# Six raw-weight buffers and three split pairs in place of four and four, in a one-core decoder layer kernel

## The chip, the cores and the metric

The kernel runs on one core of one Trainium2 chip. A time is the device time of one execution in microseconds (us). The core has a matrix engine (PE, with its weight loads listed apart as PEld), a vector engine (DVE), a scalar engine (ACT), a general engine (POOL), and a sync engine (SP) that does little but issue DMA transfers. ACT issues some transfers too.

## What is computed

One layer of a hybrid decoder, 1024 new tokens and 8 sample tokens of width 2048, in float32:

```python
mod = jax.nn.silu(c) @ w_ada + b_ada
shift, scale, gate = jnp.split(mod[:, None, :], 3, axis=-1)
h = rmsnorm(x, norm_g) * (1.0 + scale) + shift
z = h @ w_in                                   # 2048 x 8208
b_a, c_a, h_a, g_a, qkv, g_b, beta_logit, alpha_logit = jnp.split(z, SPLIT_POINTS, axis=-1)
conv_out, new_a_buf = causal_depthwise_conv(c_a * h_a, conv_a_buf, conv_a_w)
y_a = b_a * conv_out * jax.nn.silu(g_a)
...
o, s = gated_delta_rule(q, k, v, g, beta, s0)  # chunks of 64, a triangular solve in each
o = rmsnorm(o, o_norm_g).reshape(bsz, t, D_GDN).astype(x.dtype) * jax.nn.silu(g_b)
y = jnp.concatenate([y_a, o], axis=-1) @ w_out
return x + gate * y, ...                       # then a final rmsnorm
```

## The kernel before, in words

**Tiles and halves.** The tokens are taken in two halves: half 0 has 512 tokens, half 1 has 512 and the 8 samples, worked as blocks of 264 and 256 columns. In each half `h @ w_in` is made first, together with the convolution groups and the DeltaNet heads, then `@ w_out`, the residual (`res`) and the norm.

**The weight stream.** The weights come as 672 pieces of 512 rows by 128 columns (256 KB): 0 to 255 are `w_in` in half 0, 256 to 319 `w_out` in half 0, 320 to 575 `w_in` in half 1, 576 to 671 `w_out` in half 1. Class `Stream` (object `ws`, line 565 on) takes each through three steps. SP loads it into a `raw` buffer. ACT copies it to `whi` in the reduced format fp32r, and POOL or DVE (function `split_w`, which takes POOL if the planner has it free) subtracts that from `raw` into `wlo`. PE then multiplies the piece in three passes, `hh`·`whi`, `hl`·`whi` and `hh`·`wlo`, where `hh` and `hl` are the two parts of the activations (`yhi`, `ylo` in the out-projection); a piece is 12 matmuls of 512 columns, or 24 of 264 and 256; 64 pieces of the last out-projection (576 to 607 and 640 to 671) have 12 of 264 or 256 alone. `RAW` (line 391) says how many `raw` buffers there are, `SPL` how many pairs of `whi` and `wlo`. A load may be issued when it is fewer than `RAW` pieces ahead of the last split, a split when it is fewer than `SPL` ahead of the pieces that PE has finished with (method `ahead`, line 603).

**The ramp.** At the start the first two thirds of `w_ada` (shift and scale) are needed. They are 64 tiles `wat` of 512 KB, with `ADA` = 9 buffers. SP's queue issues nine of them, then `ws.ahead(0)` issues the first four raw pieces, and from then on the two kinds alternate as buffers come free. PE makes the matrix-vector products of each tile (`matvec`, tiles `tpt<-wat,sc`), `spread` transposes their result (`tpt<-cs,ev`), ACT and DVE make `hh` and `hl` of the rows that it opens, and in the waits for tiles PE does matmuls of the first 28 pieces (`first_products`, into seven PSUM tiles `mm`, `tpt`, `cht`, `ot`; `fill` takes as many as fit). While `ws.eager` is true (the ramp) the stream keeps this order; `od.spawn(ws.run())` ends it.

**The order of the work.** All instructions go through `_Order` (object `od`), a planner with a cost of each instruction and transfer; generators run beside the products (the DeltaNet `chain`, the samples, the norms) and each is continued when the planner's clock for PE reaches its due time. This runs when the kernel is built. It settles the order of the instructions on every engine, and on the chip each engine works its list in that order. So a change of the buffers also moves DVE, ACT and POOL work of other parts.

**The solve and the PSUM.** Each DeltaNet head has a triangular solve: a matrix goes to DRAM (`ub`), comes back as `tb` by a transfer that ACT issues (512 KB), and DVE does 31 steps of `ob` and `xb` with it. DVE also empties the PSUM tiles `mm` of the products (`y<-y,mm`, `ua<-c_,mm`, `res<-mm`), of which there are three; PE can't begin a product until a tile is empty.

All operations are recorded in two helpers, so every DVE, ACT, POOL and DMA row has line 321 and every matmul line 370; rows are told apart by their tiles.

Of the kernel before, what the change touches and what calls it, by code (L numbers as in the profile page):

```python
# [77 lines left out]
def trunk_kernel(tc, xT, w_in, w_ada, w_out, pack, consts, vecs, csq, ssm,  # L78
                 yT, cap, cqp, ssp, cas, cqs, sss):
    nc = tc.nc  # L80
    ctx = ExitStack()
    with ctx:
        _trunk(ctx, tc, nc, xT, w_in, w_ada, w_out, pack, consts, vecs, csq, ssm, yT, cap, cqp, ssp, cas, cqs, sss)
# [6 lines left out]
class _Order:  # L90
# [156 lines left out]
    def pump(self):  # L247
        for s in list(self.side):
            if s[0] <= self.now:
                self._step(s)  # L250
# [112 lines left out]
class _Tensor:  # L363
# [5 lines left out]
    def mm(self, out, lhsT, rhs, cost=None, **kw):  # L369
        r = self.pe.matmul(out, lhsT, rhs, **kw)  # L370
        if cost is None:
            n = _size(rhs)
            if rhs.dtype == F32R:
                cost = max(n / 2250.0, 0.05) + 0.004
            elif kw.get("is_transpose"):
                cost = 0.109
            else:
                cost = max(4 * n / 2400.0, 0.21) + 0.006
        self.od.put("P", [lhsT, rhs], [out], cost)
        return r  # L380


def _trunk(ctx, tc, nc, xT, w_in, w_ada, w_out, pack, consts, vecs, csq, ssm, yT, cap, cqp, ssp, cas, cqs, sss):
# [4 lines left out]
    def pool(name, bufs, stack=ctx, **kw):  # L388
        return _Pool(od, stack.enter_context(tc.tile_pool(name=name, bufs=bufs, **kw)), bufs)

    RAW, SPL, FX = 4, 4, 5
    cp = pool("cp", 1)
    hp = pool("hp", 4)
    yp = pool("yp", NK + 2)
# [13 lines left out]
    def ch_tile():  # L408
        return ps_g.tile([P, 512], F32, tag="ch", name="cht", bufs=2)
# [158 lines left out]
    def split_w(raw, whi, wlo):  # L568
        S.activation(whi[:], raw[:], AF.Copy)
        eng = G if od.free["G"] <= od.now + 1.0 else V  # L570
        eng.tensor_tensor(wlo[:], raw[:], whi[:].bitcast(F32), ALU.subtract)

    class Stream:
# [29 lines left out]
        def ahead(self, most=SPL):  # L603

            while True:
                if self.loaded < min(self.split + RAW, len(self.todo)):
                    raw = wp.tile([P, 4, P], F32, tag="raw", name="raw", bufs=RAW)
                    for a, b, src in self.todo[self.loaded][1]:
                        SY.dma_start(raw[:, a:b, :], src)
                    self.raws.append(raw)  # L610
                    self.loaded += 1
                elif most and self.split < min(self.freed + SPL, self.loaded) and (
                        self.eager or self.split < self.used + 2 or self.landed()):
                    whi = wp.tile([P, 4, P], F32R, tag="whi", name="whi", bufs=SPL)
                    wlo = wp.tile([P, 4, P], F32R, tag="wlo", name="wlo", bufs=SPL)
                    split_w(self.raws[self.split], whi, wlo)
                    self.raws[self.split] = None
                    self.done.append((whi, wlo))
                    self.split += 1
                    most -= 1  # L620
                else:
                    return

        def next(self, key, freed):
            assert self.todo[self.used][0] == key
            self.freed = freed
            self.ahead()
            r = self.done[self.used]
            self.done[self.used] = None
            self.used += 1  # L630
            return r
# [746 lines left out]
    ADA = 9  # L1378
# [18 lines left out]
    def busy(n):  # L1397

        n = min(n, spare[0])
        if n > 0:  # L1400
            spare[0] -= n
            t = ch_tile()
            for _ in range(n):
                mm(t[:32, :32], ones[:32, :32], ones[:32, :32], cost=0.047, start=True, stop=True)

    def fx_tile(name):
        return tp.tile([P, WH], F32, tag="fx", name=name, bufs=FX)

    def norm():

        ps = ch_tile()
        for k in range(NK):
            if k == 0:
                S.activation(acc[:, :HT], xs0[k][:, :HT], AF.Square)
                continue
            sqt = fx_tile("sqt")
            S.activation(sqt[:, :HT], xs0[k][:, :HT], AF.Square)
            if k in PSQ:
                mm(ps[:], ident, sqt[:, :HT], start=(k == PSQ[0]), stop=(k == PSQ[-1]))
            else:  # L1420
                V.tensor_tensor(acc[:, :HT], acc[:, :HT], sqt[:, :HT], ALU.add)
        V.tensor_tensor(acc[:, :HT], acc[:, :HT], ps[:], ALU.add)
        rs = rstd_of(acc, HT, None, True)
        while len(normed) < 4:
            try:
                r = next(rs)
            except StopIteration as e:
                r = None
                normed.append(e.value)
            else:  # L1430
                normed.append(r)
            yield r
# [3 lines left out]
    with ExitStack() as pools:  # L1436
# [9 lines left out]
        def load_ada():  # L1446
            if len(wats) < len(units):
                f, nf, s_, k0, nk = units[len(wats)]
                wt = ap_.tile([P, 1024], F32, tag="wa", name="wat")
                src = w_ada[k0 * P:(k0 + nk) * P, s_ * D + f * P:s_ * D + (f + nf) * P]  # L1450
                SY.dma_start(wt[:].rearrange("p (k n) -> p k n", k=nk), src.rearrange("(k p) n -> p k n", p=P))
                wats.append(wt)
# [25 lines left out]
                most -= 1  # L1478

        busy(160)  # L1480
        for _ in range(ADA):
            load_ada()
        ws.ahead(0)
        od.spawn(norm())
        pump()
        def matvec(f, nf, which, then=None):
# [443 lines left out]
```

## Time and profile before

| | |
|---|---|
| median of 3 runs | 2162.79 us (2159.91 to 2165.25) |
| the profiled execution | 2164.96 us, its span 2163.2 us |
| PE busy | 2116.0 us (98%), 15045 matmuls |
| DVE, POOL, ACT busy | 1262.9, 835.9, 826.3 us |
| moved by DMA | 299.66 MB, mean 139 GB/s |

Busy times are sums over instructions of one engine. In the timelines a row gives the start and the duration, the instruction, how many times it stands there, and in brackets how long the engine was idle just before and what ended that idle time. The clock is the share of full speed that was granted to PE.

### The profile page before, as it was taken

What the parts mean: (1) busy time and instruction counts of PE and PEld (TensorE: products, weight loads), DVE (VectorE), ACT (ScalarE), POOL (GpSimd) and SP (SyncE); (2) the same over time, 40 slices, a digit from 0 to 9 for tenths busy, and PEclk for the clock granted to TensorE, in tenths of its full rate; (3) what the DMA queues carried; (4) which work ended last, traced back from release to release, by engine and by line L of the source; (5) the groups of instructions that cost most, each with busy time, mean ns of one, the idle gap of its engine ahead of it and who ended that gap; (6) DMA issues with size and microseconds to landing.
All of it is one profiled execution on the core that took longest, in us unless ns stands there. A gap on an engine that the chain in (4) does not pass through costs nothing. (4 is left out here: it accounts for less than half of the span.)

```text
span 2163.2 us, 40436 instructions
## 1 busy us (share of the span) xinstructions
PE 2116.0 (98%) x15045; PEld 1853.8 (86%) x15045; DVE 1262.9 (58%) x3646; ACT 826.3 (38%) x1885; POOL 835.9 (39%) x808
## 2 busy tenths in 40 slices
PE   9899999999999999999999999999999999999996
PEld 6478777777788887778899999999999999999996
DVE  3347776666768645287134865666576487245454
ACT  3234343334444332343233334342443433344553
POOL 0133433333343434323444334344443433444444
PEclk9999999999999999999999999999999999999998
DMA  9974765997445357855445565467574445868776
GB/s 313 340 220 83 161 149 147 134 165 134 115 99 98 89 104 83 82 182 179 142 102 120 107 120 119 113 100 104 107 93 90 89 103 95 92 92 241 228 208 197
DMA packets 466599, 299.66 MB, mean 139 GB/s; under 512 B 37601, under 2 KB 429537, under 8 KB 466401
## 3 DMA queue, kind: packets, MB, share of 16 engines
q1 hardware_dynamic: 442608, 284.26, 61.4%
q10 hardware_dynamic: 23792, 12.81, 2.4%
q8 instruction: 118, 1.93, 0.4%
q14 instruction: 81, 0.66, 0.1%
HBM read 277.06 MB, written 19.94 MB: 137 GB/s over the span
## 5 line engine op out<-in xcount | busy, mean ns | idle before, releaser
L321 POOL TENSOR_TENSOR wlo<-raw,whi 128x512 fp32r<-128x512 f32 x536 | 718.6, 1342 | 1222.7 <-ACT whi L321 1067.6
L370 PE MATMUL mm<-hh,whi 128*128 128x264 f32 (+1 forms) x3008 | 971.6, 323 | 10.9 <-DVE y L321 5.6
L370 PE MATMUL mm<-hl,whi 128*128 128x264 f32 (+1 forms) x3008 | 969.2, 322 | 3.7 <-DVE hl L321 3.7
L370 PE MATMUL mm<-hh,wlo 128*128 128x264 f32 (+1 forms) x3008 | 968.2, 322 | 0.7 <-POOL wlo L321 0.7
L321 ACT ACTIVATE whi<-raw 128x512 fp32r<-128x512 f32 x672 | 418.4, 628 | 617.7 <-PE mm L370 323.8
L370 PEld LDWEIGHTS mm<-hh,whi 128*128 128x128 f32 x3008 | 567.7, 189 | 61.6 <-issue 9.8
L370 PEld LDWEIGHTS mm<-hl,whi 128*128 128x128 f32 x3008 | 568.0, 189 | 47.7 <-DVE hl L321 5.9
L370 PEld LDWEIGHTS mm<-hh,wlo 128*128 128x128 f32 x3008 | 567.8, 189 | 43.6 <-issue 2.5
L370 PE MATMUL mm<-yhi,wlo 128*128 128x512 f32 (+2 forms) x768 | 247.7, 323 | 5.4 <-DVE wlo L321 3.2
L370 PE MATMUL mm<-yhi,whi 128*128 128x512 f32 (+2 forms) x768 | 246.6, 321 | 1.2 <-ACT whi L321 1.2
L370 PE MATMUL mm<-ylo,whi 128*128 128x512 f32 (+2 forms) x768 | 247.1, 322 | 0.0
L321 DVE TENSOR_TENSOR ob<-tb,xb 128x62 f32<-128x62 f32 (+30 forms) x992 | 191.5, 233 | 7.0 <-DMA tb<-ub 7.0
L321 DVE TENSOR_TENSOR xb<-xb,ob 128x62 f32<-128x62 f32 (+30 forms) x992 | 195.5, 237 | 0.0
L321 DVE TENSOR_TENSOR wlo<-raw,whi 128x512 fp32r<-128x512 f32 x136 | 108.2, 802 | 110.4 <-ACT whi L321 106.3
L370 PEld LDWEIGHTS mm<-yhi,wlo 128*128 128x128 f32 x768 | 145.3, 189 | 19.9 <-DVE wlo L321 4.8
L370 PEld LDWEIGHTS mm<-yhi,whi 128*128 128x128 f32 x768 | 145.3, 189 | 12.9 <-ACT whi L321 1.7
L370 PEld LDWEIGHTS mm<-ylo,whi 128*128 128x128 f32 x768 | 145.2, 189 | 12.5 <-issue 1.0
L321 DVE SCALAR_TENSOR_TENSOR kq<-zr,pk,kq 128x512 f32<-128x512 f32 x96 | 105.0, 1094 | 3.4
L321 DVE SCALAR_TENSOR_TENSOR res<-mm,ga,xr 128x512 f32<-128x512 f32 (+2 forms) x48 | 27.3, 568 | 106.1 <-PE mm L370 92.9
L321 DVE TENSOR_TENSOR acc<-acc,sqt 128x512 f32<-128x512 f32 (+3 forms) x70 | 51.3, 736 | 38.2 <-ACT sqt L321 37.3
L321 DVE SCALAR_TENSOR_TENSOR rt<-cht,gt_neg,v 128x128 f32<-128x128 f32 x56 | 19.5, 349 | 78.9 <-PE cht L370 78.8
L321 ACT ACTIVATE u<-cht,sm 128x128 f32<-128x128 f32 x64 | 23.5, 367 | 99.6 <-DVE u L321 95.7
(410 smaller groups left out, 1996.3 us busy)
## 6 DMA issues: line engine op xcount, KB each, us to landing
raw<-in_w_in SPq DMA_DIRECT2D x488, 256.0 KB, 5.1
raw<-in_w_out SPq DMA_DIRECT2D x160, 256.0 KB, 3.3
wat<-in_w_ada SPq DMA_DIRECT2D x64, 512.0 KB, 8.7
gw<-in_w_ada SPq DMA_DIRECT2D x64, 256.0 KB, 6.5
tb<-ub ACTq DMA_DIRECT2D x16, 512.0 KB, 6.1
raw<-in_w_in SPq DMA_DIRECT2D x48, 128.0 KB, 6.7
sl<-in_ssm SPq DMA_DIRECT2D x12, 512.0 KB, 6.1
x1s<-in_xT SPq DMA_DIRECT2D x16, 260.0 KB, 4.8
```

What stands on the lines that cost most here:

```text
L321: r = f(*args, **kw)
L370: r = self.pe.matmul(out, lhsT, rhs, **kw)
```

## The change

`RAW` goes from 4 to 6, `SPL` from 4 to 3. In the ramp the limit of the loads stays at four pieces. The first four raw pieces are issued ahead of the ninth `wat` tile, not behind it.

```diff
-    RAW, SPL, FX = 4, 4, 5
+    RAW, SPL, FX = 6, 3, 5
...
-                if self.loaded < min(self.split + RAW, len(self.todo)):
+                if self.loaded < min(self.split + (4 if self.eager else RAW), len(self.todo)):
...
-        for _ in range(ADA):
+        for _ in range(ADA - 1):
             load_ada()
         ws.ahead(0)
+        load_ada()
```

A `raw` buffer takes 2 KB of a partition, as does a `whi` or a `wlo`, so the memory used stays as it is. From this the planner makes another order. Three places of it follow; the number behind a name is the instance of the tile.

First SP in the ramp, around the ninth tile (`wat_348` before, `wat_360` after):

```order
 L321 DMA wat_346<-in_w_ada 128x4x256
-L321 DMA wat_348<-in_w_ada 128x4x256
-L321 DMA raw_350<-in_w_in 128x2x128 x2
-L321 DMA raw_353<-in_w_in 128x2x128 x2
-L321 DMA raw_356<-in_w_in 128x2x128 x2
-L321 DMA raw_359<-in_w_in 128x2x128 x2
+L321 DMA raw_348<-in_w_in 128x2x128 x2
+L321 DMA raw_351<-in_w_in 128x2x128 x2
+L321 DMA raw_354<-in_w_in 128x2x128 x2
+L321 DMA raw_357<-in_w_in 128x2x128 x2
+L321 DMA wat_360<-in_w_ada 128x4x256
 L321 DMA wat_433<-in_w_ada 128x4x256
```

The four pieces have moved ahead of one tile. Further down the same queue, 23 raw pieces stood ahead of the last `wat` tile before, and 21 do now.

Next PE in the ramp, behind the first transposes of `spread`:

```order
 L370 MATMUL tpt_411<-cs_82,ev_529 128x128 x4
+L370 MATMUL tpt_568<-wat_360,sc_128 32x256 x4
+L370 MATMUL tpt_568<-wat_433,sc_128 32x256 x4
 L370 MATMUL mm_553<-hh_560,whi_536 128x512
 L370 MATMUL mm_553<-hl_561,whi_536 128x512
...
 L370 MATMUL mm_553<-hl_561,whi_536 128x512
 L370 MATMUL mm_553<-hh_560,wlo_537 128x512
-L370 MATMUL tpt_568<-wat_348,sc_128 32x256 x4
-L370 MATMUL tpt_568<-wat_433,sc_128 32x256 x4
 L370 MATMUL mm_554<-hh_560,whi_536 128x512
```

Two tiles' matrix-vector products stand ahead of the first matmuls of the products, not behind six of them. At the other end of the ramp, 87 of the 336 matmuls of `first_products` stood behind the last transposes before, and 108 do now.

Last DVE in half 1, where a convolution group's `y` is made beside a solve; before:

```order
L321 SCALAR_TENSOR_TENSOR rl_14959<-rl_14959,pk_80,rf0_10777 128x512
L321 TENSOR_TENSOR ob_15766<-tb_15691,xb_15693 128x2x16 x2
L321 TENSOR_TENSOR xb_15693<-xb_15693,ob_15766 128x2x16 x2
L321 TENSOR_TENSOR ob_15766<-tb_15691,xb_15693 128x2x15 x2
L321 TENSOR_TENSOR xb_15693<-xb_15693,ob_15766 128x2x15 x2
L321 TENSOR_TENSOR ob_15766<-tb_15691,xb_15693 128x2x14 x2
L321 TENSOR_TENSOR xb_15693<-xb_15693,ob_15766 128x2x14 x2
L321 TENSOR_TENSOR y_14333<-y_14333,mm_15806 128x264
L321 TENSOR_TENSOR y_14333<-y_14333,mm_15807 128x256
```

and of the change:

```order
L321 SCALAR_TENSOR_TENSOR gc_15772<-th_15793,gc_15772 128x520
L321 TENSOR_TENSOR y_14389<-y_14389,gc_15772 128x520
L321 SCALAR_TENSOR_TENSOR rl_14932<-rl_14932,pk_80,rf0_10775 128x512
L321 TENSOR_TENSOR y_14389<-y_14389,mm_15775 128x264
L321 TENSOR_TENSOR y_14389<-y_14389,mm_15776 128x256
L321 TENSOR_TENSOR ob_15954<-tb_15787,xb_15789 128x62 x2
L321 TENSOR_TENSOR xb_15789<-xb_15789,ob_15954 128x2x31 x2
```

The two `y<-y,mm` stood behind 36 rows of the solve (18 of its 31 steps) and now stand ahead of it. In the second group of half 1 it is the other way round: there 18 rows of a solve (9 steps), with two other rows among them, now stand right ahead of the `y<-y,mm`, where six stood.

## Rows read from the trace of the kernel before

**Rows 1.** The page: busy time, and granted clock in 40 slices

```profile
PE 2116.0 (98%) x15045; PEld 1853.8 (86%) x15045; DVE 1262.9 (58%) x3646; ACT 826.3 (38%) x1885; POOL 835.9 (39%) x808
PEclk9999999999999999999999999999999999999998
```

**Rows 2.** Stretches: length; busy PE, PEld, DVE, ACT, POOL; clock; DMA share; GB/s

```profile
0.00:140.00 140.00, 129.33 (x1082) 79.93 (x1083) 55.94 (x104) 40.26 (x64) 24.45 (x27) 0.96 1.00 319
...
926.00:1022.00 96.00, 95.83 (x413) 77.06 (x412) 78.75 (x136) 35.90 (x60) 26.82 (x19) 1.00 0.58 181
...
2100.00:2128.00 28.00, 23.78 (x175) 22.36 (x174) 21.03 (x48) 11.38 (x24) 13.55 (x10) 0.94 0.88 266
```

**Rows 3.** Waits of ACT: us in total, times, longest

```profile
ACT whi L321 <- PE mm L370: 323.8, 189, 6.7
```

**Rows 4.** Timeline of PE, ramp

```profile
37.32 0.79 PE L370 MATMUL mm<-hh,whi 128*128 128x512 f32 x1 [2.89 <-ACT hh L321]
...
141.26 1.07 PE L370 MATMUL tpt<-wat,sc 128*32 128x256 f32 x16
...
164.18 0.39 PE L370 MATMUL cht<-hh,wlo 128*128 128x512 f32 x1
164.41 0.40 PE L370 MATMUL mm<-hh,wlt 128*128 128x512 f32 x1
```

**Rows 5.** Tile `wat`, its last transfer: issue and landing

```profile
L321 SPq DMA_DIRECT2D wat<-in_w_ada x1: 419/419/419, 132.2 to 132.2; - x1
...
DMA to landing us min/median/max: 6.4/6.4/6.4
```

**Rows 6.** Timeline of ACT, end of `w_in` in half 0

```profile
905.89 0.63 ACT L321 ACTIVATE whi<-raw 128x512 fp32r<-128x512 f32 x1 [4.31 <-DMA raw<-in_w_in]
```

**Rows 7.** Timeline of PE, from there into `w_out`

```profile
912.74 0.50 PE L370 MATMUL mm<-hh,wlo 128*128 128x512 f32 x1 [0.46 <-POOL wlo L321]
...
924.01 0.49 PE L370 MATMUL mm<-yhi,wlo 128*128 128x512 f32 x1 [1.69 <-DVE wlo L321]
```

**Rows 8.** Timelines of PE and DVE, half 1, around two late `y`

```profile
1369.43 0.39 PE L370 MATMUL mm<-hh,whi 128*128 128x256 f32 x1 [1.57 <-DVE y L321]
...
1474.06 0.36 DVE L321 TENSOR_TENSOR ob<-tb,xb 128x62 f32<-128x62 f32 x2 [4.85 <-DMA tb<-ub]
...
1490.22 0.75 DVE L321 TENSOR_TENSOR y<-y,mm 128x264 f32<-128x264 f32 x2
...
1490.69 0.58 PE L370 MATMUL mm<-hh,whi 128*128 128x256 f32 x1 [4.07 <-DVE y L321]
```

**Rows 9.** Stretch just behind that stall, columns as in rows 2

```profile
1489.70:1496.50 6.80, 5.81 (x27) 5.81 (x28) 3.83 (x32) 0.63 (x1) 1.28 (x1) 0.50 0.37 80
```

**Rows 10.** Tile `tb`, issue to landing: that transfer, then all 16

```profile
DMA to landing us min/median/max: 8.8/8.8/8.8
...
DMA to landing us min/median/max: 4.5/6.1/12.0
```

**Rows 11.** Timeline of PE, `w_out` in half 1

```profile
2110.52 0.38 PE L370 MATMUL mm<-yhi,wlo 128*128 128x256 f32 x1 [1.12 <-DVE wlo L321]
2116.22 0.38 PE L370 MATMUL mm<-yhi,wlo 128*128 128x256 f32 x1 [1.15 <-POOL wlo L321]
2123.17 0.38 PE L370 MATMUL mm<-yhi,whi 128*128 128x256 f32 x1 [0.91 <-ACT whi L321]
2124.52 0.58 PE L370 MATMUL mm<-yhi,wlo 128*128 128x256 f32 x1 [0.85 <-POOL wlo L321]
...
2140.01 0.28 PE L370 MATMUL mm<-yhi,wlo 128*128 128x256 f32 x1
2140.13 0.28 PE L370 MATMUL mm<-yhi,whi 128*128 128x256 f32 x1
```

**Rows 12.** Timeline of ACT, same stretch

```profile
2118.75 0.63 ACT L321 ACTIVATE whi<-raw 128x512 fp32r<-128x512 f32 x1 [2.66 <-DMA raw<-in_w_out]
```

**Rows 13.** Timeline of ACT, `w_out` in half 0

```profile
951.84 0.82 ACT L321 ACTIVATE hh<-ht,sh,s 128x512 fp32r<-128x512 f32 x1 [3.18 <-DVE ht L321]
```

## The prediction

> **What bounds the kernel now.** The page comes first: PE is busy 2116.0 of 2163.2 us, at nearly full clock in all 40 slices [rows 1]. So there are 47 us of idle PE to win, and some time at half clock; no other engine is near its limit over the whole span. The next view is the table of stretches [rows 2], read for the idle time of PE. The first 140 us hold 10.7 us of it, and there the DMA share is 1.00: the ramp is bound by transfers. From 2100 to 2128 PE is idle for 4.2 us, with a clock of 0.94 and a DMA share of 0.88. From 926 to 1022, `w_out` in half 0, PE is busy 95.83 of 96 us, but DVE 78.75. Then the timelines say what ended each idle stretch of PE.
>
> Three places belong to the weight stream or are moved by it. At the end of `w_in` in half 0 (place B) ACT waits 4.31 us for a raw piece [rows 6] and PE then twice for a split, 0.46 and 1.69 us [rows 7]. In half 1 (place C) PE waits 4.07 us for a `y` that stands in DVE's queue behind a solve that began late, since `tb` was late [rows 8], and then runs at half clock for 6.80 us [rows 9]. In `w_out` of half 1 (place D) PE waits 1.12, 1.15, 0.91 and 0.85 us for splits [rows 11], which wait for raw pieces [rows 12].
>
> **What the buffers are worth.** ACT waits 323.8 us in all for PE to free a pair [rows 3]. That is no loss in itself: a split that can't start because all pairs are full is early. It says that the stream is mostly held by the four pairs and not by the loads. With three pairs a split can start one piece later. A piece is 12 matmuls that start 0.23 us apart [rows 4], so that is 2.8 us less lead; a short piece of the last out-projection has 12 that start 0.12 us apart [rows 11], so 1.4 us less. In return a load may run six pieces ahead of the split instead of four. Counted from the piece in use the loads reach 6+3 = 9 pieces, not 8, and a raw piece has six pieces' time to land instead of four, 16.8 us instead of 11.2. Where pieces land late this covers the lateness; where a split is late for another reason there is less cover than before.
>
> **The sum, part by part** (against the profiled 2164.96 us, which is 2.2 above the median of the runs shown).
>
> *A, the ramp.* The work of PE is the same, only its order moves, so only its idle time counts. SP's queue has two raw pieces (2 × 0.26 MB) fewer ahead of the last `wat` tile; at 319 GB/s [rows 2] that brings the tile 1.6 us forward. It was issued at 132.2 and landed 6.4 us later, at 138.6 [rows 5], and its matrix-vector product started only at 141.26 [rows 4]: PE was 2.7 us behind the transfer, with work in hand. The 21 matmuls that move behind the last transposes (108 instead of 87) take 21 × 0.23 = 4.9 us out of what PE does before, so without new idle time it would be there at 136.4. With the tile landing at 137.0 it waits 0.6 us; were the tile no earlier, 2.2 us. At the other end the two tiles' products that stand ahead of the first `mm` now can fill part of the 2.89 us for which PE waits there for `hh` [rows 4]. But the second of them needs the tile that now comes 4 × 0.26 MB = 1.05 MB, 3.3 us, later. I take 1.2 us of gain there and 0.6 us of loss at the end: **−0.6**, between −2.5 (the gap filled, no wait at the end) and +2.2.
>
> *B.* The lateness is of loads: 4.31 us, well inside the 5.6 us by which a piece now has longer. Both waits go: 0.46 + 1.69 = **−2.1**, between −2.1 and 0.
>
> *C.* `y<-y,mm` no longer stands behind 18 steps of the solve, so the late `tb` doesn't hold it. The 4.07 us go, and with them the half clock: 5.81 us of matmuls [rows 9] would have taken 2.9 less. **−7.0**, between −7.0 and 0.
>
> *D.* Loads and splits are both late here. ACT waited 2.66 us for a piece [rows 12], and two more pieces of load lead cover that in a stage where a piece takes 2.8 or 1.4 us. But DMA is 0.88 busy, and one pair less takes away the reserve of POOL and DVE. The idle is 4.0 us, the clock 28 × 0.06 = 1.7 us [rows 2]. I take half of the idle and the fall of the clock: 2.0 + 1.7, less 0.2 for a new small wait, **−3.5**, between −5.7 and +2.
>
> *E, one pair less.* Where PE waits now for no split, the lead of most splits is several times 1 us, and 2.8 us less still leaves some. It doesn't in two stretches. In `w_out` of half 0 ACT's queue has the copies behind the `hh` of the next half, which waits 3.18 us for DVE's `ht` [rows 13]; a copy that is queued there comes that much late, and the reserve of the pairs was what hid it. If it had 0.7 us to spare, it now comes 2.8 − 0.7 = 2.1 us late. I count that once, since DVE's own work, 78.75 of 96 us [rows 2], then falls back by as much as PE and the next product finds it where it was. In the short pieces of half 1 one such wait of about 1.4 us is likely. Together **+3.6**; from below 0, if the earlier loads give the reserve back; from above 10, five such waits.
>
> Sum: −0.6 − 2.1 − 7.0 − 3.5 + 3.6 = −9.6, which gives 2164.96 − 9.6 = 2155.4, so **2155**.
>
> A rule speaks against it. In place C the transfer of `tb` took 8.8 us, where the median of the 16 is 6.1 and the longest 12.0 [rows 10]. The Trainium skill ("DMA: Bandwidth & Descriptors", section "Issuing engines are not separate DMA queues") says that transfers issued by different engines run on the same 16 DMA engines and interleave, so six raw pieces in flight would slow `tb`, where four did. The spread from 4.5 to 12.0 agrees that it doesn't have the DMA engines to itself, and no run here shows what six do. By that rule the time would be that of the returned stall below, 2162.4.
>
> Another rule reads rows 3 the other way. The Trainium skill ("Perfetto Trace Analysis", section "Optimization Strategy") takes the same gap again and again, on the engine that should be saturated, for a sign of too few buffers; the 323.8 us are ACT's, which needn't be saturated, and PE's 47 us come in single places. By that rule the pairs would not be the shortage, E would be near 0, and the sum 2151.8.
>
> **The rivals.**
>
> *The stall of C comes back elsewhere.* The planner's order is a new one for the whole program, and it doesn't know which `tb` will be late. In the second group of half 1, `y<-y,mm` now stands behind 18 rows of the solve where six stood, and it stalled PE for 1.57 us already [rows 8]. In place C the 36 rows and three longer instructions took 1490.22 − 1474.06 = 16.2 us, some 0.4 us a row, so 12 rows more are 4.9 us; with the clock's fall as in C that is about 7. For it: it decides as soon as one `tb` of 16 is late by more than some 3 us, and six raw pieces share the DMA engines with it. Against it: the solves that have no `y` behind them absorb it. The time is 2155.4 + 7 = 2162.4.
>
> *The three pairs bind in `w_out` of half 0 (slower).* DVE's `res` empties the product, then `ht` and `hh` follow, the copies are queued behind `hh`, and the next product waits for the split. If DVE and ACT are tied to PE in that way, the loss of 2.1 us doesn't come once but at each of the eight products for which half 1's `hh` is being made: 8 × 2.1 = 17. It decides where the reserve of a split is below 2.8 us. For it: 78.75 of 96 us of DVE, and the 3.18 us for `ht`. Against it: the other 17 us of DVE let it catch up between products. The time is 2155.4 + 17 = 2172.
>
> *PE waits for the last tile of the ramp and loses its clock.* If the last tile isn't earlier, PE waits 2.2 us; with half clock behind it for some 3 us of matmuls, 1.5 more. The time is 2155.4 + 0.6 + 3.7 − 0.6 = 2159.
>
> *The solves and chains come better too.* PE has other waits of 1 to 1.6 us, like the 1.57 us of rows 8, of which a new order may miss four: 2155.4 − 6 = 2149.
>
> **How the numbers follow.** About 0.3%, 6.5 us, is what a measurement of this kernel can tell from no change: 2156.3 and 2169.3 are its bounds around the median. The forecast gets 0.38 (its own range 2150 to 2160, by the bounds of A, B and D), the returned stall 0.29, the slower case 0.14, the ramp 0.09, the better chains 0.10. Below 2156.3 lie all of the last and some nine tenths of the forecast: 0.44. Above 2169.3 lies the slower case, 0.14; the rest is 0.42. A range from 2147 to 2167 leaves out the slower case and a little of the others.
>
> **What would show it.** Right: PE's timeline has no wait above 0.5 us for a split between 905 and 930 and none for `y` at the place of C; ACT's wait for raw pieces falls, and its wait for PE to free a pair rises above 323.8 us; the first `hh`·`wlt` matmul stays within 2 us of 164.41. Wrong: waits of PE for `wlo` or `whi` at a regular distance of one product between 926 and 1022 (the pairs), a `tb` above 9 us with a stall of `y` or `ua` behind it (the returned stall), or waits of PE for `wat` around 136 with clock 0.50 behind them (the ramp).

## The result, and the profile after

The change takes 2147.43 us (median of 4 runs, 2143.82 to 2149.42) where the kernel before took 2164.02 beside it: a ratio of 0.9921, 95% interval 0.9908 to 0.9934. That is 16.6 us. In a second comparison, below, it was 0.9935 (0.9922 to 0.9948). The gain is real and about twice the 7.8 us by which the forecast of 2155 lay below the median of before, 2162.79. One execution of all those below, among the twelve of e6, took 7238.51 us, and the ratio of e6 leaves it out.

The page of the change, parts 1 and 2, beside [rows 1]:

```profile
span 2147.6 us, 40476 instructions
...
PE 2108.6 (98%) x15045; PEld 1851.5 (86%) x15045; DVE 1252.4 (58%) x3635; ACT 832.6 (39%) x1885; POOL 849.0 (40%) x819
...
PEclk8999999999999999999999999999999999999998
```

PE is idle for 2147.6 − 2108.6 = 39.0 us instead of 47.2, and its own busy time is 7.4 us less for the same 15045 matmuls. Three places lost a half-clock stretch or an idle one, and one was added.

The waits of ACT for raw pieces, first before (beside its wait for PE in [rows 3]) and then of the change, with both reasons (us in total, times, longest):

```profile
ACT whi L321 <- DMA raw<-in_w_in: 123.0, 50, 8.0
...
ACT whi L321 <- DMA raw<-in_w_out: 36.2, 24, 3.1
```

```profile
ACT whi L321 <- PE mm L370: 473.5, 273, 3.8
...
ACT whi L321 <- DMA raw<-in_w_in: 11.7, 5, 3.1
ACT whi L321 <- DMA raw<-in_w_out: 11.3, 6, 3.1
```

ACT waited 159.2 us for raw pieces and now waits 23.0. What it waits for instead is PE, which must free a pair. Now the stretches of the change, columns as in [rows 2]; the first is place B, the third and fourth are places C and D, which come earlier now:

```profile
905.00:926.00 21.00, 21.00 (x92) 16.97 (x91) 13.16 (x17) 14.20 (x26) 7.28 (x6) 1.00 0.75 153
926.00:1022.00 96.00, 94.86 (x408) 76.23 (x408) 73.30 (x130) 37.04 (x59) 29.16 (x21) 1.00 0.57 178
1475.00:1490.00 15.00, 15.00 (x128) 15.00 (x127) 8.16 (x35) 3.80 (x6) 7.11 (x5) 1.00 1.06 165
2088.00:2116.00 28.00, 24.66 (x205) 24.02 (x204) 20.51 (x50) 14.02 (x27) 15.21 (x10) 1.00 0.95 277
```

At B (905 to 926) PE is busy all the time; at C too, with full clock; at D (2088 to 2116) some idle time remains, but no half clock. The longest waits of PE for splits in these stretches, against [rows 7, 11]:

```profile
943.50 0.51 PE L370 MATMUL mm<-yhi,wlo 128*128 128x512 f32 x1 [1.15 <-POOL wlo L321]
...
2109.77 0.39 PE L370 MATMUL mm<-yhi,wlo 128*128 128x256 f32 x1 [2.09 <-POOL wlo L321]
```

Of the six waits, 6.2 us in all, one is left, at place D. The one of 1.15 us is new: before, PE had no wait above 0.2 us from 926 to 1022, in `w_out` of half 0. DVE at place C, against [rows 8], and its `tb`, against [rows 10]:

```profile
1482.26 0.43 DVE L321 TENSOR_TENSOR y<-y,mm 128x264 f32<-128x264 f32 x1 [5.83 <-PE mm L370]
```

```profile
DMA to landing us min/median/max: 11.1/11.1/11.1
```

DVE now waits for PE there, not PE for DVE. The `tb` of this head took 11.1 us, more than the 8.8 of before, but no `y` stands behind it. Another stall is new, in `w_in` of half 0:

```profile
345.99 0.38 PE L370 MATMUL tpt<-sp 128*128 128x256 f32 x1 [2.62 <-ACT sp L321]
```

PE waits 2.62 us for an `sp` that stands in ACT's queue behind a transfer (`yc<-xd`) that itself waits for another (`xd<-xb`) to land; ACT is idle for 5.21 us there, and no split is what it waits for.

### The profile page after: what moved, and what is told of

Same layout as the page of the kernel before. It is cut to its first block, busy times and chain, and to the rows that moved or that the text cites. A ratio compares the mean times of both kernels' runs of the same rounds, so it can differ in the third digit from the quotient of the medians.

```text
span 2147.6 us, 40476 instructions
## 1 busy us (share of the span) xinstructions
PE 2108.6 (98%) x15045; PEld 1851.5 (86%) x15045; DVE 1252.4 (58%) x3635; ACT 832.6 (39%) x1885; POOL 849.0 (40%) x819
## 4 chain that ended last, share of the span: by engine, by line
PE 52%; DVE 2%; DMA 1%; POOL 0%; issue 0%; ACT 0%; POOLq 0%; ACTq 0%; DVEq 0%
PE mm L370 48%; PE cht L370 2%; PE tpt L370 1%; DVE xb L321 1%; PE ot L370 1%; DVE ob L321 0%; DMA tb<-ub 0%; DVE kq L321 0%; POOL wlo L321 0%; DMA ub<-dU 0%; POOL res L321 0%; DVE sl L321 0%; DVE y L321 0%; DVE wlo L321 0%; DMA xr<-in_xT 0%
## 5 line engine op out<-in xcount | busy, mean ns | idle before, releaser
L321 POOL TENSOR_TENSOR wlo<-raw,whi 128x512 fp32r<-128x512 f32 x547 | 731.4, 1338 | 1204.6 <-ACT whi L321 1026.9
L321 ACT ACTIVATE whi<-raw 128x512 fp32r<-128x512 f32 x672 | 421.2, 629 | 686.3 <-PE mm L370 473.5
L321 DVE TENSOR_TENSOR ob<-tb,xb 128x62 f32<-128x62 f32 (+30 forms) x992 | 200.7, 242 | 3.6 <-DMA tb<-ub 3.6
L321 DVE TENSOR_TENSOR xb<-xb,ob 128x62 f32<-128x62 f32 (+30 forms) x992 | 202.6, 244 | 0.0
L370 PEld LDWEIGHTS mm<-yhi,wlo 128*128 128x128 f32 x768 | 144.5, 188 | 16.6 <-POOL wlo L321 3.9
L321 DVE TENSOR_TENSOR wlo<-raw,whi 128x512 fp32r<-128x512 f32 x125 | 89.2, 715 | 58.8 <-ACT whi L321 58.3
L321 DVE TENSOR_TENSOR acc<-acc,sqt 128x512 f32<-128x512 f32 (+3 forms) x70 | 56.8, 816 | 32.0 <-ACT sqt L321 31.2
```

Source lines behind the costliest of these rows:

```text
L321: r = f(*args, **kw)
```

## The experiments

Two theories stood after the result. **L**: the gain is the lead of the loads. **O**: it is a lucky order of the planner, most of it DVE's order at place C. Between them stood the question whether the third pair had cost what the prediction charged.

The table gives the length of stages in each profile, in us; the pieces are found by counting PE's matmuls with `whi` or `wlo`, 12 or 24 to a piece. A stage reaches from the first matmul of one piece to the first of another (28 to 252 is the rest of half 0's `w_in` without its end, 252 to 264 is place B, 264 to 320 the rest of `w_out` in half 0, 428 to 576 holds place C, 576 to the end holds D).

| raw, pairs | kernel | to 28 | 28–252 | 252–264 | 264–320 | 320–428 | 428–576 | 576–end | span |
|---|---|---|---|---|---|---|---|---|---|
| 4, 4 | before | 171.8 | 737.0 | 37.1 | 165.5 | 350.6 | 484.3 | 216.8 | 2163.2 |
| 4, 4 | e2 moved tile alone | 172.1 | 735.0 | 37.3 | 165.5 | 350.4 | 482.6 | 215.0 | 2158.0 |
| 4, 4 | e9 other order | 174.8 | 734.4 | 38.8 | 165.7 | 350.2 | 481.9 | 217.6 | 2163.5 |
| 4, 4 | e11 other order | 172.2 | 741.5 | 33.4 | 165.1 | 348.9 | 483.3 | 214.9 | 2159.3 |
| 4, 4 | e16 solve later | 174.9 | 734.7 | 36.6 | 165.6 | 350.4 | 481.7 | 215.1 | 2159.1 |
| 4, 4 | e5 17 `y` buffers | 170.5 | 734.6 | 39.3 | 167.1 | 351.9 | 484.5 | 217.3 | 2165.3 |
| 5, 4 | e6 same order, fifth raw | 170.5 | 734.7 | 35.1 | 167.2 | 351.9 | 485.1 | 215.0 | 2159.5 |
| 4, 3 | e3 | 173.6 | 735.3 | 33.6 | 165.2 | 350.5 | 484.5 | 219.3 | 2162.1 |
| 5, 3 | e4 | 176.1 | 739.0 | 33.7 | 166.8 | 354.1 | 485.0 | 213.3 | 2168.0 |
| 6, 3 | the change | 173.3 | 737.6 | 35.0 | 165.0 | 349.6 | 476.5 | 210.6 | 2147.6 |
| 6, 3 | e13 the change again | 169.7 | 737.4 | 35.0 | 165.0 | 348.3 | 476.5 | 211.9 | 2143.7 |
| 6, 3 | e1 without the move | 172.4 | 736.5 | 35.0 | 165.0 | 349.2 | 476.7 | 211.9 | 2146.6 |
| 6, 3 | e14 without the move, again | 174.9 | 736.8 | 35.0 | 165.0 | 349.4 | 476.5 | 210.6 | 2148.2 |
| 6, 3 | e18 no limit in the ramp | 174.8 | 737.2 | 35.0 | 165.0 | 348.4 | 476.5 | 212.1 | 2148.9 |
| 6, 3 | e15 17 `y` buffers | 169.4 | 736.3 | 38.6 | 165.7 | 350.2 | 478.4 | 213.6 | 2152.2 |
| 6, 3 | e10 other order | 173.6 | 742.5 | 34.1 | 165.3 | 349.6 | 477.9 | 211.9 | 2154.8 |
| 6, 3 | e12 other order | 173.5 | 736.3 | 35.6 | 165.0 | 347.1 | 478.5 | 211.9 | 2147.8 |
| 8, 2 | e17 | 180.3 | 757.5 | 37.1 | 169.0 | 356.3 | 490.9 | 227.2 | 2218.2 |

### One part at a time

e1, the change without the moved tile:

```diff
-        for _ in range(ADA - 1):
+        for _ in range(ADA):
             load_ada()
         ws.ahead(0)
-        load_ada()
```

> Six raw buffers and three pairs, with the raw loads behind the ninth w_ada tile as before. Theory L (the gain is the longer lead of the loads): the gain stays, 2144 to 2149 us, and ACT's wait for raw pieces stays below 40 us (it was 159 before, 23 after). Theory O (the gain is a lucky order of DVE around the stall at 1490 us, the lead is worth little): the order is new again, so 2150 to 2164. Theory R (the nine tiles and the ramp carry it): back to 2160 to 2165. The ramp should end 1 to 2 us earlier than with the moved tile, where the first logits matmul came at 165.9 instead of 164.4.

It took 2152.62 us, ratio 0.9953 (0.9940 to 0.9965); ACT waited 18.6 us for raw pieces. Most of the gain stays, though the time lies above the range of L and within that of O; e14, below, is the same kernel again.

e2, the kernel before with the moved tile and nothing else (the diff of the change's last part alone):

> Four and four buffers as before, only the ninth w_ada tile behind the first four raw loads. L: no gain, 2164 to 2167, with the ramp 1.5 us longer and ACT's wait for raw pieces at 140 to 180 us. O: the order is new as well, so the stall of 4 us may go: 2153 to 2167. R: 2150 or less.

2161.22 us, 0.9993 (0.9984 to 1.0002), with 143.4 us of waits for raw pieces: no gain, and the stall at C is 3.7 us.

e3, before with three pairs:

```diff
-    RAW, SPL, FX = 4, 4, 5
+    RAW, SPL, FX = 4, 3, 5
```

> Four raw buffers, three pairs, ninth tile as before. L: the lead of the loads falls by a piece (seven instead of eight), ACT's wait for raw pieces stays at 120 to 200 us, and the waits of PE for splits at 905 to 926 and 2100 to 2128 are 1 to 5 us longer in all: 2165 to 2173. A theory S, that three pairs cost what the prediction charged (3.6 us) and more with the short lead: 2168 to 2180. O: 2153 to 2170, without a clear sign.

2163.95 us, 1.0006 (0.9998 to 1.0015): not to be told from before, and below what L expected (and S, that three pairs cost what was charged). The stage on which the prediction charged 2.1 us, 264 to 320, took 165.2 us, where before it took 165.5. From 576 on three pairs with four raw buffers did cost 219.3 − 216.8 = 2.5 us in this one profile; the four other orders with four and four in the table have 214.9 to 217.6 there.

e4, five raw buffers and three pairs, without the moved tile (the loads' limit in the ramp stays at four, as in the change):

```diff
-    RAW, SPL, FX = 6, 3, 5
+    RAW, SPL, FX = 5, 3, 5
```

> Five raw buffers, three pairs, ninth tile as before. The raws reach eight pieces beyond the piece in use, as before, but a piece has five pieces' time to land instead of four. L: if the time to land matters, half of the gain, 2152 to 2158; if the reach matters, 2163 to 2168. O: 2150 to 2168, without order between this, e1 and e3.

2165.86 us, 1.0017 (1.0008 to 1.0027). The time is that of L's second case, in which the reach of the loads counts, and it lies in the wide range of O. But if too short a reach had held the loads back, ACT would still wait for raw pieces:

```profile
ACT whi L321 <- DMA raw<-in_w_out: 7.3, 6, 2.4
ACT whi L321 <- DMA raw<-in_w_in: 6.3, 3, 2.9
```

These waits have fallen to 13.6 us, lower than with six, and no time came of it in the whole. In the table the stages that hold B and D are shorter than before, by 3.4 and 3.5 us, as a longer lead would make them; the ramp, 28 to 252, 264 to 320 and 320 to 428 are longer by 4.3, 2.0, 1.3 and 3.5 (the profile is that of the slowest of its 11 executions). And at place C nothing changed; PE's row there:

```profile
1498.40 0.58 PE L370 MATMUL mm<-hh,whi 128*128 128x256 f32 x1 [4.20 <-DVE y L321]
```

The wait for the late `y` is as long as before. So most of ACT's wait for loads was in itself no loss; what it cost PE stood, as far as the table shows, at B and D.

### The same order, other buffers

For these the planner is told of the same buffers as before (or as in the change), so the order is the same instruction for instruction, and the real number of buffers is another. Memory is full, so a buffer of `y` is given up for a raw one. e5 and e6:

```diff
-    yp = pool("yp", NK + 2)
+    yp = pool("yp", NK + 2, real=NK + 1)
...
-                    raw = wp.tile([P, 4, P], F32, tag="raw", name="raw", bufs=RAW)
+                    raw = wp.tile([P, 4, P], F32, tag="raw", name="raw", bufs=RAW, real=5)
```

(e5 has the first of the two edits alone. `real` is a new parameter, which gives the allocation another number of buffers than the planner; PE, DVE, POOL and SP have the same instructions in the same order in the traces of before, e5 and e6.)

> The order of before, instruction for instruction, with 17 buffers of y instead of 18; a control for the next run. L and O: the same as before, 2162 to 2167, unless a y has to wait for its buffer.

> The order of before, instruction for instruction, and 17 buffers of y; the buffer freed is a fifth raw buffer, of which the planner doesn't know. Only the chip's loads run one piece further ahead. L: ACT's wait for raw pieces falls from 159 to 60 to 110 us, the stalls of PE for splits at 905 to 926 and 2100 to 2128 (2.2 and 4.0 us, and 1.7 us of clock) fall by half or more: 2156 to 2161; the stall for y at 1490 stays, about 4 us. O: 2162 to 2167.

e5 took 2169.2 us, 1.0033 (1.0020 to 1.0046): the missing `y` buffer costs some 7 us. e6 took 2163.99, 1.0007 (0.9998 to 1.0015). Between the two only the fifth raw buffer differs, and it is worth 5.2 us. (By the time alone e6 lies in the range of O; that range was set without the cost of the `y` buffer.) The waits of ACT, e5 and then e6:

```profile
ACT whi L321 <- DMA raw<-in_w_in: 111.1, 46, 8.3
ACT whi L321 <- DMA raw<-in_w_out: 26.8, 20, 3.0
```

```profile
ACT whi L321 <- DMA raw<-in_w_in: 31.4, 16, 9.9
ACT whi L321 <- DMA raw<-in_w_out: 20.4, 15, 3.7
```

In the table, place B falls by 4.2 us and the last stage by 2.3; 428 to 576 doesn't fall. That is what the loads' lead alone does: it mends B and D, and leaves C.

e7, e8 and e15 do the same with the order of the change: 17 buffers of `y` (e15), with a seventh raw buffer (e7), or with a fourth `whi` (e8).

> The order of the change, instruction for instruction, 17 buffers of y, and a seventh raw buffer. L: little is left to win, ACT's wait for raw pieces falls from 23 to below 15 us, 2145 to 2149. A theory D, that deeper loads slow the transfers of tb: tb's median above 6.5 us and 2149 to 2155.

> The order of the change, instruction for instruction, 17 buffers of y, and a fourth whi buffer (wlo stays at three). ACT's copies may run a piece further ahead; the subtraction stays. If three pairs cost something here (the prediction charged 3.6 us), some of it comes back: 2143 to 2146, and the stalls for splits at 943 and 2110 (1.2 and 2.1 us) shrink. If they cost nothing: 2147 to 2149, with both stalls as they are.

> The order of the change with 17 buffers of y and nothing else: the control for the runs with a seventh raw buffer (2152) and a fourth whi (2157). In the order of before a missing y buffer cost 7 us. If the third pair cost something, this is slower than the run with the fourth whi, over 2160; if it costs nothing, the two agree, 2152 to 2158. If deeper loads still helped, this is over 2154.

e15 took 2156.74 us, 0.9976 (0.9966 to 0.9986), e8 2157.25, 0.9981 (0.9971 to 0.9990): the fourth `whi` is worth nothing, so with six raw buffers ACT's copies are not short of a buffer. Yet ACT's wait for PE fell from 486.5 us in e15 to less than half in e8:

```profile
ACT whi L321 <- PE mm L370: 211.9, 110, 5.8
```

It went on to POOL, whose wait for PE ahead of `wlo` rose from 66.7 to 421.8 us. (A fourth `wlo` would not fit and wasn't tried.) e7 took 2152.18, 0.9956 (0.9940 to 0.9971), perhaps 4 us better than e15, in another comparison; a `y` buffer is worth more than a seventh raw. The median `tb` took 6.3 us in e7, so theory D, slower transfers of `tb`, finds no support.

With 17 buffers of `y` throughout, the steps are 2169.2 us (e5), 2164.0 with a fifth raw buffer in the same order (e6), and 2156.7 with six, three pairs and the order made for them (e15, in another comparison). The first step, 5.2 us, is the loads' lead alone. The second, 7.3 us, isn't parted: it holds a sixth buffer, one pair less and the order. The order of the change with fewer than six raw buffers wasn't tried: in that order a load in SP's queue would come to wait for a buffer that only later work frees.

### What another order is worth

e9 and e10 change one margin of the planner, before and in the change; e11 and e12 another:

```diff
-MARGIN, LAND = 0.6, 2.0
+MARGIN, LAND = 0.6, 2.2
```

> Four and four as before; in the planner alone the margin that it gives a transfer to land is 2.2 us instead of 2.0, which makes another order and changes nothing else. It measures what an order is worth. L: 2158 to 2168, without the lead no order reaches the change. O: the spread is wide, and the stall at 1490 goes or moves: 2150 to 2172.

> The change, with that margin at 2.2 us. L: 2143 to 2152. O: 2150 to 2172, in the same band as the run with four and four.

> Four and four as before; in the planner alone the margin of generators that wait for another engine is 0.7 us instead of 0.6, again only another order. L: 2158 to 2168. O: 2150 to 2172.

> The change, with that margin at 0.7 us. L: 2143 to 2152. O: 2150 to 2172.

With four and four: 2161.45 us, 1.0001 (0.9991 to 1.0011), and 2161.96, 0.9997 (0.9986 to 1.0008). With six and three: 2154.25, 0.9965 (0.9956 to 0.9975), and 2147.1, 0.9928 (0.9910 to 0.9947). Theory O wanted both in one band; e10 lies 2 us above the range of L. Other orders with four and four gain nothing, and every order made with six and three gains. But the two bands also show that an order is worth up to 7 us within the same buffers.

The stall for `y` goes with the buffers as well. PE's row at place C in e11, with four and four:

```profile
1489.09 0.58 PE L370 MATMUL mm<-hh,whi 128*128 128x256 f32 x1 [3.38 <-DVE y L321]
```

In every kernel whose order was made for four or five raw buffers, but for e16, it is there with 2.7 to 4.2 us; in none made for six is a stall over 0.9 us at that place. e16 takes it away with four and four:

```diff
         yield LANDED
+        for _ in range(36 if (half, h) == (1, 3) else 0):
+            yield 0.3
         ot = gp.tile([P, 4, 31], F32, tag="ob", name="ob", bufs=1)
```

> Four and four buffers as before; in half 1 the solve of the fourth head alone is held back by 10.8 us of the planner's clock, so that y<-y,mm stands behind 3 steps of it instead of 18. If the order there is what the gain in half 1 is made of: the stall of 4 us at 1490 and the half clock behind it go, that stage (pieces 428 to 576, 483 us before, 477 with the change) falls to 476 to 479, and the time is 2154 to 2158, with the waits for raw pieces as before. If the stall only hid another wait: 2160 to 2164, and the stage stays above 481.

2160.89 us, 0.9997 (0.9987 to 1.0007), the second of the two cases. The stall is gone, but the stage from 428 to 576 only fell from 484.3 to 481.7 us. Counted over that stage, PE is still idle for 4.2 us (5.7 before, 1.1 in the change), 2.7 us of it between pieces 512 and 544, most of that in waits for results of DVE (`st`, `sx`, `rt`). So it isn't the one stall that makes the stage; in this order PE waits for other results a little later.

### The moved tile, two pairs, and the ramp

e13 and e14 are the change and e1 again, side by side.

> The change itself, again, beside the next run on the same chip. If the moved ninth tile adds to the gain, this is 3 to 7 us faster than the next run; if not, the two agree within 2 us, since their profiles (2147.6 and 2146.6 us of span) have the same stages but for 1 us of ramp. 2146 to 2152.

> Six and three without the moved tile, again. 2146 to 2152, and the same as the change within 2 us, if the move is worth nothing; 2150 to 2155 if it is worth what the first runs seem to say.

2147.1 us, 0.9935 (0.9922 to 0.9948), and 2148.86, 0.9942 (0.9930 to 0.9954): the moved tile is worth nothing that can be told.

e17, eight raw buffers and two pairs, and e18, the change without the limit of four loads in the ramp:

```diff
-                if self.loaded < min(self.split + (4 if self.eager else RAW), len(self.todo)):
+                if self.loaded < min(self.split + RAW, len(self.todo)):
```

> Eight raw buffers and two pairs, ninth tile as before, in the same memory. If pairs were never short, 2145 to 2152, as with six and three. If the reserve ends between three and two pairs, PE waits for splits all over: with two pairs a split has one piece's time, 2.8 us, for 0.63 us of copy and up to 1.3 us of subtraction and their queues; the short pieces with 1.4 us can't be fed: 2170 to 2250, most of it in pieces 576 to 607 and 640 to 671 and in w_out of half 0.

> The change with six loads ahead in the ramp too. More raw pieces ahead of the last w_ada tile: the tile lands later and PE waits for it, or has more products to fill with. If the ramp is bound by the tiles: 1 to 5 us slower than the change, 2148 to 2154. If PE's own work sets the ramp's end: the same within 2 us, 2146 to 2150.

e17 took 2220.14 us, 1.0269 (1.0255 to 1.0283). Two rows of its waits:

```profile
PE mm L370 <- POOL wlo L321: 20.0, 48, 0.8
...
PE mm L370 <- DVE wlo L321: 7.4, 13, 1.3
```

PE waits 61 times for a `wlo`, 8 times before. It is idle for 72.6 us and busy for 2145.6, 33.6 and 37.0 us more than in the change, for as many matmuls. The loss isn't where it was expected, mostly in the short pieces and `w_out` of half 0: those from 576 on and 264 to 320 have 20.6 of the 70.6 us, 28 to 252 has 19.9 and 428 to 576 has 14.4. ACT's wait for PE is 473.3 us in e17 and 473.5 in the change: the same number beside a time that is 73 us longer. e18 took 2151.31, 0.9955 (0.9942 to 0.9969): its five executions (2150.87 to 2154.34) lie above the ten of the change (2143.82 to 2149.84), but these were other comparisons, and the interval overlaps that of e13. From piece 28 on its stages are those of e13 within 0.3 us; the ramp is 5.1 us longer, and as long as in e14, which has the limit. That the limit is worth some 4 us is not shown.

## Why the prediction was right or wrong

**The sum.** 2155 was forecast and 2147.43 measured, inside the range and at its edge. Against the profiled execution the sum was −9.6; the two spans differ by 15.6. The direction and the places were right, the size was not.

**E, one pair less, is the step that failed.** The prediction charged 2.1 us in `w_out` of half 0, since a copy "comes that much late", and 1.4 in the short pieces (3.5 together; its sum has 3.6). Measured by stages: −0.5 from 264 to 320 (165.0 against 165.5), and −1.6 from 576 to 640 (146.2 against 147.8). E was +3.6 and came out at −2.1, 5.7 of the 6.0 us by which the sum is off. That the rest is so small is luck: against their terms A is off by +2.1, C by −0.8, D by −1.1, and the stages without a term by −0.4.

Waits of the kind that E charges did come, but smaller. In `w_out` of half 0 three copies stood in ACT's queue behind an `hh` that waited for DVE's `ht`:

```profile
939.71 0.82 ACT L321 ACTIVATE hh<-ht,sh,s 128x512 fp32r<-128x512 f32 x1 [2.44 <-DVE ht L321]
...
940.95 1.65 ACT L321 ACTIVATE whi<-raw 128x512 fp32r<-128x512 f32 x3
```

PE then waited the 1.15 us at 943.50 that are shown above, once (it is piece 263, so the stage from 252 to 264 holds it), and in the short pieces 0.67 us at 1942.48. That is 1.8 us, half of what was charged, and the stages became shorter in spite of them. e3 shows that the charge was wrong by itself: three pairs with the old loads left the stage from 264 to 320 as it was, and PE has no wait above 0.2 us for a split in all of `w_out` in half 0, so the wait at 943.50 needn't come from the pair that is gone. In the short pieces there was a cost, up to 2.5 us in e3, and with six raw buffers and their order it is gone; that is the end of the range named as "the earlier loads give the reserve back". And e17 shows that the reserve isn't endless: with two pairs, and eight raw buffers, PE has 61 waits. The step from four pairs to three was free within what can be told; eight and two instead of six and three costs some 70 us.

**A, the ramp,** was −0.6; the first logits matmul came at 165.87 instead of 164.41 [rows 4]. But the profile of the same kernel in e13 has its ramp (to piece 28) 3.6 us shorter, so nothing of this size can be read from one profile. The gap of 2.89 us for `hh` was partly filled, as predicted (1.90 us are left), but a wait of 2.27 us for `hl` stands behind it now. e2 and the pair e13, e14 say that the move does nothing that can be told.

**B** was −2.1 and the stage from 252 to 264 is 2.1 us shorter, with E's wait of 1.15 us in it; the waits of before are gone. The cause is partly shown: e6, with nothing but a fifth raw buffer, shortens it too; but in e3 and e11 it is short without one, so an order can do the same.

**C** was −7.0 and the stage from 428 to 576 is 7.8 us shorter: the size was right, the mechanism too simple. The late `y` did go, as predicted, and the half clock with it. But e16 takes away the same stall for 2.6 us in the stage and nothing in the time. All profiles in the table with six and three have this stage at 476.5 to 478.5, those with four and four at 481.7 to 484.5. Why the planner's orders for six raw buffers let PE through there, and those for four or five don't, is open; no run separates it from the order.

**D** was −3.5. From piece 640 to the end the profile is 4.6 us shorter (64.4 against 69.0); four waits of 4.0 us became one of 2.09, and the clock stays at 1.00. That the clock stays is luck of this profile: in e13, with the same order, the same wait took 2.10 us, the granted clock of the next 3.4 us was 0.52, and from 640 on it took 65.6 us, 1.2 more.

**The rivals.** The three pairs did not bind in `w_out` of half 0; 926 to 1022 has a PE busy 94.86 of 96 us, with one wait of 1.15 us and not one at each product. The stall of C did not come back in the second group of half 1: 1.48 us where 1.57 stood. The sentence that transfers of different engines interleave (the Trainium skill, "DMA: Bandwidth & Descriptors", section "Issuing engines are not separate DMA queues") agrees with the 11.1 us of `tb` in place of 8.8 at this one place, but the time did not follow, since DVE had no `y` behind it. Over all 16 `tb` it isn't borne out: their median is 6.5 us, and 5.6 to 6.8 in the kernels with four raw buffers; and at this place, in the order of the change, seven raw buffers have 9.1 (e7) where six have 10.9 (e15). Of the other rule, on repeated gaps (the Trainium skill, "Perfetto Trace Analysis", section "Optimization Strategy"), the sum would have been 2151.8; it was nearer than 2155.4, and e17 shows the repeated gaps on PE that it speaks of.

**Fairly set,** the means of the five kernels with four and four buffers (before, e2, e9, e11, e16) and of five profiles with six and three (the change, e13, e1, e10, e12) differ by 12.5 us of span: 1.7 at B, 5.5 from 428 to 576, 4.3 from 576 on, 1.3 from 320 to 428, 0.4 and 0.7 in two others, and 1.5 lost from 28 to 252. So about half of the gain, B and the end, is where e6 has the loads' lead shorten a stage, and nearly as much is in the stage whose cause is open. The change has one of the best orders of its kind; e12's 2147.1 equals it, and none of the kernels run beats it clearly.

## What to carry to other kernels

A producer's wait for its consumer to free a buffer says only that it is early; how many buffers it needs is read from the consumer's waits for it, and from a run with one buffer fewer. A wait of an engine off the critical path can vanish (159 us to 14 in e4) or move to another engine (e8) without a gain in the time, so a change of prefetch is best tried with the order of all else held fixed, as in e5 and e6. Where a planner makes the order, run two or three orders of each setting before a few us are put down to the setting.

## What the runs showed that was not expected

The ramp of one and the same kernel does not repeat: up to piece 28 it took 173.3 and 169.7 us in two profiles of the change, and 172.4 and 174.9 in two of the kernel without the moved tile, while the stage from 428 to 576 was 476.5 in both of the change. In both pairs most of the difference of the spans arises in the first 175 us.
